# Splitting thirteen of sixteen output weight pieces in the retention and value stages of a transformer layer, with the value products grouped by high and low parts

## The chip, the cores and the metric

The kernel runs on one core of one Trainium2 chip. The metric is the device time of one execution in microseconds (us). Before the change it was measured three times: 1208.9, 1209.09 and 1209.12, median 1209.09 us.

A core has five engines with instruction streams of their own: TensorE (PE in the profile: matmuls and transposes; PEld is its loading of weights), VectorE (DVE), ScalarE (ACT), GpSimd (POOL) and SyncE (SP), which here only issues transfers. Each engine takes its instructions in the order in which they are written for it, and waits on semaphores for what the others make.

## The reference

One decoder layer over 1024 positions of width 1024, in float32. Eight heads of width 64 do causal softmax attention with a forget gate, four heads of width 128 do retention; their outputs are joined, projected by `w_out`, and a gated MLP follows.

```python
h = x * (1.0 + sc1) + sh1
proj = h @ w_in[l]
fq, fk, fv, ff, rq, rk, rv, rg = jnp.split(proj, IN_SPLITS, axis=-1)
log_f = jax.nn.log_sigmoid(ff + b_f[l])
fox = forgetting_attention(fq, fk, fv, log_f)     # softmax(q k^T * scale + cum_i - cum_j), causal
ret = retention(rq, rk, rv, rg)                   # chunks of 128, normalised, times silu(g)
mix = jnp.concatenate([fox, ret], axis=-1) @ w_out[l]
x = layer_norm(ALPHA * x + g1 * mix, ln1_g[l], ln1_b[l])
h = x * (1.0 + sc2) + sh2
u = causal_depthwise_conv(h @ w_up[l], conv_w[l], conv_b[l])
a, bv = jnp.split(u, 2, axis=-1)
y = (jax.nn.gelu(a, approximate=False) * bv) @ w_down[l]
x = layer_norm(ALPHA * x + g2 * y, ln2_g[l], ln2_b[l])
```

## The kernel before

**Split products.** A float32 product is made of several matmuls in a shorter float32 type (fp32r). An operand is split into a high part, which is the operand cast to that type, and a low part, which is the operand minus the high part; the product is high by high, high by low and low by high. The cast is usually ScalarE's and the subtraction VectorE's. So each weight that is used in this way costs one operation on each of the two engines before TensorE can have it.

**Stages.** In order of time: the first products of retention (to 49 us), the retention heads (to 222), the value projection of attention together with the forget gates (to 272), forgetting attention ("fox", eight heads, to 484), the output projection and the first normalisation (to 595), the up projection (to 989) and the down projection (to 1207).

**Retention and value stage.** A head of retention is worked through in eight chunks of 128 rows; the loop runs over `m`, the number of head and chunk together. For each chunk TensorE makes the projection (24 matmuls of 512 columns, tile rp), and between these the steps of earlier chunks are emitted: the turned queries and keys (qkT, copied by ScalarE at L434; `turned["last"]` is the last such copy), their products (pS), the decay on VectorE, the output (po), normalisation, gate, and the outputs turned back (py). They are copied by ScalarE into yt (L523) and stored to `mixR` in DRAM (L525). The value stage has sixteen quarter steps `q`, each for one block of rows and one half of the columns (tile vp); ScalarE casts the high part of the values (L698), VectorE subtracts (L699). At `q` = 8 the log of the forget gates is made on VectorE by a series (L710 to L734, result lp), at 12 it is summed by TensorE (pcum), at 13 it is turned (pcumT), split and stored to `cum_d` (L761), from where GpSimd loads it into the keys of attention (tile kc, L663).

These two stages are written inside one block that a scheduler orders by a simulated timeline; what is not fixed by data or by hand may move. `vec` and `queued` fix the order among VectorE's retention operations and some transfers; `tc.issue_after(x)` puts an instruction behind `x` on its engine. Memory comes from pools of slots: tag "S" has three slots of 4 KB per partition, of which retention uses two (trig and dec), "T" four of 2 KB.

**Forgetting attention.** A head has eight row blocks, `i`. For each one TensorE makes the scores (ps, L833 and L834), VectorE takes a running minimum (L836), ScalarE the exponentials (L843), GpSimd divides (L847), TensorE turns the result back in pieces of 128 by 128 (pt, L901), ScalarE casts the high part of the probabilities (L909) and VectorE subtracts the low part (L910). `fox_pv` multiplies these with the values in three groups of row blocks, at `i` = 2, 5 and 7 with a lag of four steps (pv, L921): a group runs over its key blocks `kb`, and for each over the parts `u`, high and low, so that the two alternate. In between, TensorE makes the projections of queries and keys for the next head (qk, L800 to L802), which ScalarE (L806, L807, L815) and VectorE (L808, L812, L816) turn into the operands qq, kk and kc, and the next weights are split (L674 and L675). The order of all this is the order in which the loop over `s_` calls the parts.

**Output weights.** `w_out` has eight row blocks of 1024 columns. It is split ahead of its use, in sixteen pieces of 128 by 512, `PIECES`: a piece is loaded (L1065), ScalarE casts the high part (L1069), VectorE subtracts in place (L1076), and two stores (L1082) put both parts into the DRAM tiles `wod`, from which `wo_load` takes them in the last head. All sixteen are done during attention. `LOWS` gives the step at which a piece's subtraction and stores come: row blocks 3 and 5 of the first seven heads, and row block 0 of heads 3 and 5 (counted from 0) as well; the load comes four steps earlier, the cast two. The cast is issued behind the last exponential, the subtraction behind the last minimum.

Of the kernel before, what the change touches and what calls it, by code (L numbers as in the profile page):

```python
# [8 lines left out]
F32 = mybir.dt.float32  # L9
# [6 lines left out]
P = 128  # L16
# [15 lines left out]
def kernel(  # L32
# [172 lines left out]
    first = [fa[0][:, :512], fa[0][:, 512:], fa[1][:, :512], fa[1][:, 512:]]  # L205
    first += [bank(f"fb{i}") for i in range(3)]
    w0 = []
    mod1 = cp.tile([P, ND, 2], F32, tag="mod1", name="mod1")

    hs = {}  # L210

    def ret_consts():
        tr = slot("S", [P, 2, NT, 64], F32, "trig")
        queued("SP", nc.sync.dma_start, tr, trig)
        rc = cp.tile([P, 3, RH], F32, tag="rc", name="rc")
        queued("SP", nc.sync.dma_start, rc, rcols)
        w1_load(2)
        dec = slot("S", [P, RH, P], F32, "dec")
        queued("SP", nc.sync.dma_start, dec, decay)
        w1_load(3)  # L220
        bfb = cp.tile([P, FH], F32, tag="bfb", name="bfb")
        queued("SP", nc.sync.dma_start, bfb, bcast_rows(b_f, FH))
        lnc = cp.tile([P, 2, ND], F32, tag="lnc", name="lnc")
        queued("SP", nc.sync.dma_start, lnc, ln1_cols)
        cw = cp.tile([P, 2 * NFF, 4], F32, tag="cw", name="cw")
        return tr, dec, rc, bfb, lnc, cw

    def h_cuts(j):
# [285 lines left out]
    def ret_out(h, half, st):  # L514
        pt = bank(f"py{h}_{half}")
        for i in range(4):
            c = half * 4 + i
            turn(
                pt[:, i * P:(i + 1) * P], st["st"][c // 2][:, c % 2, 0:P], ident
            )  # L520
        for q in range(2):
            yt = tmp([P, 256], F32, f"yt{h}_{half}_{q}")
            nc.scalar.copy(yt, pt[:, q * 256:(q + 1) * 256])  # L523
            s0 = half * 512 + q * 256
            nc.sync.dma_start(mixR[h, :, s0:s0 + 256], yt)  # L525

# [71 lines left out]
    def mod_piece():  # L598
        n = mst.get("n", 0)
        m, j = divmod(n, ND)  # L600
        if m < 4:
# [2 lines left out]
            mod_part(m, j, a)  # L604
            mst["n"] = n + 1

    ret_state(0)
    for c in range(7):
        ret_rows(0, c, first[c], sts[0])
# [6 lines left out]
    for m in range(NT - 1, RH * NT):  # L616
# [17 lines left out]
            mod_piece()  # L634
        if m > 2 * NT and c == 1:
            mod_piece()
        if m == NT + 1:
            mod_load(0)
        if 0 < h < RH - 1 and 3 <= c < 7:
# [123 lines left out]
    for q in range(2 * NT):  # L763
        n, c = 1 - q // NT, q % NT
        v_proj(c, n)
        emit(2 * RH * NT + q)
        if q < 8:
            mod_piece()
        if q in (2, 10):
            mod_rows(q // 8)  # L770
        if q == 3:
            wqk = [slot("X", [P, ND, P], F32R, f"wq{n}") for n in "hl"]
            fox_load(0)
            for half in range(2):
                fox_w(0, half)
        if q == 8:
            Lp = log_forget()
        if q == 12:
            cum = cum_forget(Lp)
        if q == 13:  # L780
            cum_store(cum)
        if q == 14:
            fox_load(1)
            fox_consts()
        if q == 15:
            T = {0: fox_alloc(0)}
# [125 lines left out]
    def fox_pv(h, g):  # L912
# [1 line left out]
        i0, i1 = SPANS[g]  # L914
        pts = PT.pop((h, g))
        pv = bank(f"pv{h}_{g}")
        for kb in range(i1 + 1):
            q0 = min(max(kb, i0), i1 - 1)
            t, at_ = where(g, kb, q0)
            for u in range(2):  # L920
                nc.tensor.matmul(  # L921
                    pv[:, (q0 - i0) * P:(i1 + 1 - i0) * P], V2[h][:, kb, :],
                    pts[t][u][:, at_:at_ + (i1 + 1 - q0) * P],
# [130 lines left out]

    wod = [dp.tile([2, P, D], F32, tag=f"wod{m}", name=f"wod{m}") for m in range(ND)]
    PIECES = [(m, slice(n, n + 512)) for m in (4, 5, 6, 7, 0, 1, 2, 3) for n in (0, 512)]
    park, wo = {}, {}

    def park_load(k):
        if k < len(PIECES):
# [129 lines left out]

    LAG = 3

    LOWS = [NT * h + i for h in range(FH - 1) for i in ((0, 3, 5) if h in (3, 5) else (3, 5))]
    LOWS = {v: k for k, v in enumerate(LOWS)}
    LOADS = {0: (4, 5), 1: (6, 7), 2: (0, 1), 3: (2, 3)}
    for part in range(4):
        fox_proj(0, T[0], 0, part)
# [697 lines left out]
```

## Time and profile before

| what | before |
|---|---|
| runs, median | 1209.09 us |
| the profiled execution | 1209.29 us |
| its span | 1207.6 us |
| TensorE busy | 1194.3 us, 99% |
| VectorE busy | 917.1 us, 76% |
| ScalarE busy | 653.2 us, 54% |
| GpSimd busy | 239.1 us, 20% |
| granted clock of TensorE | 0.998 |
| moved by DMA | 212.54 MB |

The span is the part of the execution that the profile covers; 1.69 us lie around it. "Busy" is the share of time in which an engine has an instruction at work. For TensorE this overstates the use: matmuls are pipelined and their ends are modelled, so that a stop of a few tenths of a microsecond between two matmuls can vanish under the end of the first. Such a stop is seen when starts are compared: a matmul of 512 columns is normally followed 0.23 us later. In the rows of the profile, `out<-in` are the program's tiles with their numbers left out, `x16` is a count, and in square brackets stands the idle time before an instruction and who ended it.

### The profile page before, as it was taken

The numbers are of one execution on the slowest core, as the hardware profiler recorded it, in microseconds if no ns is written. First come the engines' busy times: TensorE is split into PE (matmuls) and PEld (weight loads), VectorE is DVE, ScalarE is ACT, GpSimd is POOL, SyncE is SP. The second block draws the span as 40 slices with busy tenths as digits, with TensorE's granted clock in tenths as the row PEclk, the third lists the DMA queues.
The fourth block names the chain that finished last, engine by engine and source line by source line (L and its number), as shares of the span: only waits on it lengthen the run. The fifth ranks groups of instructions, "written<-read, shape, count | busy, mean of one in ns | idle before, by whom it ended". The sixth has DMA issues, their size and how long they took to land.

```text
span 1207.6 us, 17130 instructions
## 1 busy us (share of the span) xinstructions
PE 1194.3 (99%) x5928; PEld 1000.6 (83%) x5928; DVE 917.1 (76%) x1765; ACT 653.2 (54%) x1220; POOL 239.1 (20%) x283
## 2 busy tenths in 40 slices
PE   9999999999999999999999999999999999999997
PEld 6788888998888888888888888888888888888886
DVE  8947657767888886467998778787787876886687
ACT  6635445346777776657764545445454555543452
POOL 0015345122433343000021322211100010000021
PEclk9999999999999999999999999999999999999999
DMA  9523444613455568222278978777454489975741
GB/s 361 227 88 127 129 148 148 202 52 128 133 167 158 187 204 325 90 95 96 88 194 215 208 184 194 177 189 174 138 139 131 150 245 286 333 248 181 255 175 70
DMA packets 93511, 212.54 MB, mean 176 GB/s; under 512 B 10760, under 2 KB 17240, under 8 KB 93424
## 3 DMA queue, kind: packets, MB, share of 16 engines
q1 hardware_dynamic: 80496, 188.27, 44.8%
q0 software_dynamic: 12928, 23.17, 11.9%
q8 instruction: 47, 0.77, 0.2%
q14 instruction: 40, 0.33, 0.1%
HBM read 169.35 MB, written 76.65 MB: 204 GB/s over the span
## 4 chain that ended last, share of the span: by engine, by line
PE 92%; DVE 3%; DMA 2%; ACT 2%; issue 1%; SPq 0%; DVEq 0%; ACTq 0%
PE rp L145 11%; PE dX L1582 9%; PE dZ L1582 7%; PE uX L1358 6%; PE uX L1356 6%; PE uX L1357 6%; PE uY L1358 5%; PE uY L1357 5%; PE uY L1356 5%; PE vp L145 4%; PE pv L921 3%; PE op L184 2%; PE op L182 2%; PE op L183 2%; PE pt L901 2%; DMA ada<-in_ada_dram 2%
## 5 line engine op out<-in xcount | busy, mean ns | idle before, releaser
L145 PE MATMUL rp<-wr,hhi 128*128 128x512 f32 x400 | 127.9, 401 | 0.0
L1568 DVE TENSOR_TENSOR dl<-dr,dh 128x1024 fp32r<-128x1024 f32 x66 | 80.7, 1238 | 33.5 <-ACT dh L1556 30.9
L1185 POOL DMA_DIRECT2D sd<-gd x22 | 18.1, 821 | 396.8 <-DMA sd<-y 226.1
L847 POOL TENSOR_TENSOR S<-S,dn 128x128 f32<-128x128 f32 (+3 forms) x64 | 76.6, 1207 | 100.1 <-DVE dn L846 65.3
L1556 ACT CAST dh<-dr 128x1024 fp32r<-128x1024 f32 x58 | 59.9, 1051 | 64.0 <-DMA dr<-td 31.1
L145 PEld LDWEIGHTS rp<-wr,hhi 128*128 128x128 f32 x400 | 71.6, 189 | 12.7
L145 PE MATMUL rp<-wr,hlo 128*128 128x512 f32 x200 | 78.4, 392 | 0.0
L843 ACT ACTIVATE S<-S,mn 128x128 f32<-128x128 f32 (+3 forms) x64 | 49.9, 780 | 29.1 <-DVE mn L836 28.5
L1582 PE MATMUL dX<-dh 128*128 128x512 f32 x165 | 64.2, 389 | 0.0
L1582 PE MATMUL dX<-dl,dh 128*128 128x512 f32 x165 | 64.2, 389 | 0.0
L1582 PE MATMUL dX<-dh,dl 128*128 128x512 f32 x165 | 64.2, 389 | 0.0
L1371 ACT COPY u<-uX 128x512 f32<-128x512 f32 x44 | 25.8, 587 | 70.3 <-PE uX L1358 70.3
L145 DVE CUSTOM_DVE_ANT_0 ada<-ada,csb,cb 128x1024 f32<-128x1024 f32 x46 | 60.0, 1309 | 3.2 <-DMA ada<-in_ada_dram 2.7
L910 DVE TENSOR_TENSOR pt<-pt,pt 128x384 fp32r<-128x384 f32 (+3 forms) x104 | 50.9, 517 | 6.6 <-ACT pt L909 6.1
L800 PE MATMUL qk<-hhi,wqh 128*128 128x512 f32 x128 | 53.4, 417 | 0.0
L1582 PE MATMUL dZ<-dh 128*128 128x512 f32 x132 | 51.6, 391 | 0.0
L801 PE MATMUL qk<-hlo,wqh 128*128 128x512 f32 x128 | 51.5, 402 | 0.0
L1582 PE MATMUL dZ<-dl,dh 128*128 128x512 f32 x132 | 51.4, 389 | 0.0
L1582 PE MATMUL dZ<-dh,dl 128*128 128x512 f32 x132 | 51.4, 389 | 0.0
L802 PE MATMUL qk<-hhi,wql 128*128 128x512 f32 x128 | 51.1, 399 | 0.0
L182 PE MATMUL op<-wo,mxs 128*128 128x512 f32 x128 | 50.8, 397 | 0.0
L184 PE MATMUL op<-wo,mxs 128*128 128x512 f32 x128 | 50.1, 391 | 0.0
(1080 smaller groups left out, 3667.9 us busy)
## 6 DMA issues: line engine op xcount, KB each, us to landing
ada<-in_ada_dram SPq DMA_DIRECT2D x48, 512.0 KB, 3.8
td<-in_w_down_dram SPq DMA_DIRECT2D x44, 256.0 KB, 5.2
wa<-in_w_up_dram SPq DMA_DIRECT2D x22, 512.0 KB, 4.7
wb<-in_w_up_dram SPq DMA_DIRECT2D x22, 512.0 KB, 4.0
gd<-y SPq DMA_DIRECT2D x22, 512.0 KB, 2.7
sd<-y SPq DMA_DIRECT2D x44, 256.0 KB, 3.2
dr<-sd SPq DMA_DIRECT2D x44, 256.0 KB, 3.8
dr<-td SPq DMA_DIRECT2D x44, 256.0 KB, 4.2
```

The lines of the kernel that those rows point to most:

```text
L145: order[key] = fn(*args, **kw)
L182: mm(pt, ahi, whi, start=start, stop=False)
L184: mm(pt, alo, whi, start=False, stop=stop)
L800: nc.tensor.matmul(pt, whi[:, j, :], hhi[j][:, sl], start=(j == 0), stop=False)
L801: nc.tensor.matmul(pt, whi[:, j, :], hlo[j][:, sl], start=False, stop=False)
L847: nc.gpsimd.tensor_tensor(out=Ssb[:, :span], in0=Ssb[:, :span], in1=den.to_broadcast([P, span]), op=ALU.mult,)
L1356: nc.tensor.matmul(pt, whi, bh, start=start, stop=False, skip_group_check=True)
L1357: nc.tensor.matmul(pt, whi, bl, start=False, stop=False, skip_group_check=True)
L1358: nc.tensor.matmul(pt, wlo, bh, start=False, stop=stop, skip_group_check=True)
L1556: nc.scalar.copy(hi, raw)
L1568: nc.vector.tensor_tensor(out=lo, in0=raw, in1=f(hi), op=ALU.subtract)
L1582: nc.tensor.matmul(pt[:, to or cols], w_[:, 0, q], m_[:, 1, cols], start=start and n_ == 0, stop=stop and n_ == 2, skip_group_check=True)
```

## The change

There are three edits.

1. The splitting of pieces 0 to 12 moves from attention into the retention and value stages. `early_parks(n)` is called once per chunk from `m` = 9 on and once per quarter step `q`, so `n` runs from 0 to 38; every three calls make one piece: load, then cast and subtraction, then the two stores. They use one buffer, the third slot of tag "S", for all thirteen pieces. The cast is issued behind the last turned query, the subtraction is queued among VectorE's retention operations. `LOWS` keeps the last three pieces, at row block 5 of head 5 and row blocks 3 and 5 of head 6.
2. In `fox_pv` the loops over the part `u` and the key block `kb` are exchanged: all products of a group with high parts come first, then all with low parts.
3. In `ret_out` the copies to yt are issued behind the last turned query.

```diff
 def ret_consts():
+        park["ret"] = slot("S", [P, 2, 512], F32, "park")
 def ret_out(h, half, st):
             yt = tmp([P, 256], F32, f"yt{h}_{half}_{q}")
-            nc.scalar.copy(yt, pt[:, q * 256:(q + 1) * 256])
+            with tc.issue_after(turned["last"].ins):
+                nc.scalar.copy(yt, pt[:, q * 256:(q + 1) * 256])
...
+    def early_park(k, step):
+        m, sl = PIECES[k]
+        t = park["ret"]
+        if step == 0:
+            nc.sync.dma_start(t[:, 1, :], w_out[m * P:(m + 1) * P, sl])
+        elif step == 1:
+            with tc.issue_after(turned["last"].ins):
+                nc.scalar.copy(t[:, 0, :].bitcast(F32R), t[:, 1, :])
+            vec(nc.vector.tensor_tensor, out=t[:, 1, :].bitcast(F32R), in0=t[:, 1, :],
+                in1=t[:, 0, :], op=ALU.subtract)
+        else:
+            for u in range(2):
+                nc.sync.dma_start(wod[m][u][:, sl], t[:, u, :])
+
+    def early_parks(n):
+        k, step = divmod(n, 3)
+        if k < EARLY:
+            early_park(k, step)
+
+    EARLY = 13
...
+        if m > NT:
+            early_parks(m - NT - 1)
...
         emit(2 * RH * NT + q)
         if q < 8:
             mod_piece()
+        early_parks((RH - 1) * NT - 1 + q)
...
         pv = bank(f"pv{h}_{g}")
-        for kb in range(i1 + 1):
-            q0 = min(max(kb, i0), i1 - 1)
-            t, at_ = where(g, kb, q0)
-            for u in range(2):
+        for u in range(2):
+            for kb in range(i1 + 1):
+                q0 = min(max(kb, i0), i1 - 1)
+                t, at_ = where(g, kb, q0)
                 nc.tensor.matmul(
...
-    LOWS = [NT * h + i for h in range(FH - 1) for i in ((0, 3, 5) if h in (3, 5) else (3, 5))]
-    LOWS = {v: k for k, v in enumerate(LOWS)}
+    LOWS = {v: EARLY + n for n, v in enumerate((NT * 5 + 5, NT * 6 + 3, NT * 6 + 5))}
```

The rest of the diff only moves the definitions of `wod`, `PIECES` and `park` ahead of the block.

On VectorE the subtraction of a piece now stands among the retention and value operations, where it did not before (rst and V are retention rows and values, vp the value products, ada and gcol a row sum of the modulation). After the change, in the value stage:

```order
L728 TENSOR_TENSOR V_6_2441<-vp_1_2542,V_6_2441 128x64
L145 TENSOR_TENSOR park<-park 128x512
L145 SCALAR_TENSOR_TENSOR rst_3_1859<-rst_3_1859 128x128
L728 TENSOR_TENSOR V_4_2439<-vp_1_2597,V_4_2439 128x64
L145 ISA ada_3_3_2587,gcol<-ada_3_3_2587,csb,cb 128x1024
```

It stands between values of two quarter steps. The places in attention and on SyncE's queue are shown in the prediction.

More of the change, by code (lines that the diff above doesn't have):

```diff
@@ L207 @@
     w0 = []
+    wod = [dp.tile([2, P, D], F32, tag=f"wod{m}", name=f"wod{m}") for m in range(ND)]
+    PIECES = [(m, slice(n, n + 512)) for m in (4, 5, 6, 7, 0, 1, 2, 3) for n in (0, 512)]
+    park = {}
     mod1 = cp.tile([P, ND, 2], F32, tag="mod1", name="mod1")
@@ L1053, in h2_split @@
         return low
-    wod = [dp.tile([2, P, D], F32, tag=f"wod{m}", name=f"wod{m}") for m in range(ND)]
-    PIECES = [(m, slice(n, n + 512)) for m in (4, 5, 6, 7, 0, 1, 2, 3) for n in (0, 512)]
-    park, wo = {}, {}
+    wo = {}
     def park_load(k):
```

## Prediction

> **What bounds the kernel now.** The page of the profile comes first: its header, its table of busy time and the first line of its chain.
>
> ```profile
> span 1207.6 us, 17130 instructions
> PE 1194.3 (99%) x5928; PEld 1000.6 (83%) x5928; DVE 917.1 (76%) x1765; ACT 653.2 (54%) x1220; POOL 239.1 (20%) x283
> PE 92%; DVE 3%; DMA 2%; ACT 2%; issue 1%; SPq 0%; DVEq 0%; ACTq 0%
> ```
>
> TensorE is the bound nearly everywhere, and the change takes no matmul away. It can only win or lose at the places where TensorE stands still, and a busy share of 99% doesn't show those, because the modelled ends of matmuls cover short stops. So I read the busy time stage by stage, then the distance between starts. In the view by windows the columns after the stretch are its length and then PE, PEld, DVE, ACT and POOL busy (with counts), clock, DMA share and GB/s.
>
> ```profile
> 52.00:120.00 68.00, 68.00 (x369) 58.38 (x368) 44.57 (x149) 28.46 (x85) 23.16 (x34) 1.00 0.29 93
> 222.00:272.00 50.00, 50.00 (x420) 49.96 (x419) 35.66 (x155) 20.16 (x86) 9.55 (x15) 1.00 0.35 117
> 272.00:484.00 212.00, 210.70 (x1180) 177.89 (x1180) 174.36 (x471) 150.33 (x357) 80.43 (x71) 1.00 0.56 185
> ```
>
> The rows are a stretch of retention, the value stage and forgetting attention. VectorE is 82% busy in attention (174.36 of 212.00) and 66 and 71% in the others; ScalarE is 71% there against 42 and 40%. Attention is also the only one of these stages in which TensorE isn't covered. The granted clock is 1.00 in all rows.
>
> What TensorE waits for in attention at the value products (L921) is asked of that line; the rows give microseconds of idle time, counted on the loading of weights, and how often:
>
> ```profile
>   DVE pt L910: 3.1, 8
>   ACT pt L909: 2.3, 7
> ```
>
> These 5.4 us bound what faster probability pieces can give at L921; part of a late weight load is covered by the matmul ahead of it.
>
> **The change part by part.** *Thirteen pieces leave attention.* The work moved is that of the tile park:
>
> ```profile
> L1065 SPq DMA_DIRECT2D park<-in_w_out_dram x16: 333/482/1218, 268.6 to 419.4; - x16
> L1069 ACT CAST park<-park x16: 602/606/628, 283.0 to 438.2; 128x512 fp32r<-128x512 f32 x16
> L1076 DVE TENSOR_TENSOR park<-park,park x16: 674/778/1339, 288.9 to 442.0; 128x512 fp32r<-128x512 f32 x16
> DMA to landing us min/median/max: 2.0/3.3/6.5
> ```
>
> A piece costs VectorE 0.78 us and ScalarE 0.61 us at the median. Thirteen take 10.1 us and 7.9 us out of attention. None of that is TensorE time; it counts where a subtract stands ahead of a low half that TensorE awaits. The first order shows this on VectorE, from the low halves of the seventh row block of the second head (pt_7; park is L1076, a running minimum of the scores is an ISA row). Before:
>
> ```order
> L808 SCALAR_TENSOR_TENSOR qq_3555<-qk_1_3725,qq_3555 64x512
> L910 TENSOR_TENSOR pt_2_0_1_3804<-pt_7_0_3842,pt_2_0_0_3803 128x4x128
> L910 TENSOR_TENSOR pt_2_1_1_3806<-pt_7_1_3849,pt_2_1_0_3805 128x4x128
> L812 TENSOR_TENSOR kc_3557<-qk_1_3725,kk_3556 64x512
> L816 CAST kk_3556<-kk_3556 64x512
> L675 TENSOR_TENSOR wql<-wqkr_3625,wqh 128x512
> L836 ISA S_3_3881,mn_3_3882<-ps_3_3883,late 128x512
> L836 ISA mn_3_3882 128x1
> L1076 TENSOR_TENSOR park_1_3733<-park_1_3733,park_0_3732 128x512
> ```
>
> After the change the same place reads:
>
> ```order
> L940 TENSOR_TENSOR pt_2_0_1_3835<-pt_7_0_3873,pt_2_0_0_3834 128x4x128
> L940 TENSOR_TENSOR pt_2_1_1_3837<-pt_7_1_3880,pt_2_1_0_3836 128x4x128
> L876 RECIPROCAL dn_2_3869<-dn_2_3869 128x1
> L919 MEMSET pt_0_0_0_3940 128x128
> L919 MEMSET pt_0_0_1_3941 128x128
> L838 SCALAR_TENSOR_TENSOR qq_3600<-qk_1_3763,qq_3600 64x512
> L842 TENSOR_TENSOR kc_3602<-qk_1_3763,kk_3601 64x512
> L846 CAST kk_3601<-kk_3601 64x512
> L704 TENSOR_TENSOR wql<-wqkr_3666,wqh 128x512
> L866 ISA S_3_3912,mn_3_3913<-ps_3_3914,late 128x512
> ```
>
> The subtract is gone, and the two low halves that the third group of value products needs now stand ahead of the turned query (qq). On TensorE the same place, up to those products (pv_2), reads before:
>
> ```order
> L834 MATMUL ps_3_3883<-kc_3557,q_0_3099 128x512
> L901 MATMUL pt_7_1_3849<-ident,S_7_3713 128x128 x4
> L800 MATMUL qk_0_3874<-hhi_162,wqh 128x512
> L801 MATMUL qk_0_3874<-hlo_178,wqh 128x512
> L802 MATMUL qk_0_3874<-hhi_162,wql 128x512
> L800 MATMUL qk_0_3874<-hhi_182,wqh 128x512
> L801 MATMUL qk_0_3874<-hlo_223,wqh 128x512
> L802 MATMUL qk_0_3874<-hhi_182,wql 128x512
> L921 MATMUL pv_2_3895<-pt_2_0_0_3803,V_1_2389 128x256
> L921 MATMUL pv_2_3895<-pt_2_0_1_3804,V_1_2389 128x256
> ```
>
> and after it:
>
> ```order
> L830 MATMUL qk_0_3905<-hhi_190,wqh 128x512
> L831 MATMUL qk_0_3905<-hlo_231,wqh 128x512
> L832 MATMUL qk_0_3905<-hhi_190,wql 128x512
> L863 MATMUL ps_3_3914<-kk_3601,qq_3600 128x512
> L864 MATMUL ps_3_3914<-kc_3602,q_0_3171 128x512
> L951 MATMUL pv_2_3922<-pt_2_0_0_3834,V_1_2436 128x256 x4
> L951 MATMUL pv_2_3922<-pt_2_1_0_3836,V_1_2436 128x256 x4
> L951 MATMUL pv_2_3922<-pt_2_0_1_3835,V_1_2436 128x256 x4
> L951 MATMUL pv_2_3922<-pt_2_1_1_3837,V_1_2436 128x256 x4
> ```
>
> A pair of score products now stands between the projection and pv_2, and the low halves come after eight high products. What each place costs is read from five pieces of the chain of waits (start, length, what) in heads without and with the stop, and from the timeline of TensorE, VectorE and GpSimd (start, length).
>
> ```profile
> 309.22 2.18 PE pv L921 x16
> 318.35 0.83 PE pv L921 x6
> 343.23 1.08 PE pv L921 x6
> 359.61 1.92 PE pv L921 x16
> 434.30 2.19 PE pv L921 x16
> ```
>
> ```profile
> 393.16 0.81 PE L921 MATMUL pv<-pt,V 128*128 128x384 f32 x2
> 443.26 0.82 PE L921 MATMUL pv<-pt,V 128*128 128x384 f32 x2
> 349.22 1.68 POOL L847 TENSOR_TENSOR S<-S,dn 128x896 f32<-128x896 f32 x1 [2.87 <-DVE dn L846]
> 350.17 1.28 DVE L1076 TENSOR_TENSOR park<-park,park 128x512 fp32r<-128x512 f32 x1
> 351.44 0.40 DVE L910 TENSOR_TENSOR pt<-pt,pt 128x256 fp32r<-128x256 f32 x1
> 351.30 0.40 PE L801 MATMUL qk<-hlo,wqh 128*128 128x512 f32 x1
> 351.53 0.39 PE L802 MATMUL qk<-hhi,wql 128*128 128x512 f32 x1
> 351.99 0.41 PE L921 MATMUL pv<-pt,V 128*128 128x384 f32 x1
> 352.24 0.34 PE L833 MATMUL ps<-kk,qq 128*128 128x384 f32 x1
> 352.41 0.34 PE L834 MATMUL ps<-kc,q 67*128 67x384 f32 x1
> 401.60 0.39 PE L802 MATMUL qk<-hhi,wql 128*128 128x512 f32 x1
> 402.12 0.41 PE L921 MATMUL pv<-pt,V 128*128 128x384 f32 x1
> ```
>
> - Third group, sixteen products: 2.18 against 1.92, so 0.26 us, in four of the eight heads, the first at 309.22 and the last at 434.30: 4 × 0.26 = 1.04. The new order covers it with a pair of score products and earlier low halves; I take 0.9, from 0 (the next wait takes its place) to 1.0.
> - First group, six products, where the second is already a low one: 1.08 against 0.83, so 0.25 us. In two more heads the first two products, at 393.16 and 443.26, take 0.81 where 0.17 + 0.34 = 0.51 is due: three heads, 0.75. With high parts first the first low product is the fourth one, which covers the stop even in the seventh head, whose piece stays. I take 0.6, from 0 to 0.75.
> - Second group: a 512-column product normally starts 0.23 us after the one before (351.30 to 351.53), but the value product came 0.46 later, and it then took 0.25 (351.99 to 352.24) where 384 columns take 0.17 (352.24 to 352.41). That is 0.31 us, behind a subtract of 1.28 us, whose end released the low half at 351.44. It happens in two heads (351.53 to 351.99, and 0.52 from 401.60 to 402.12), those with three pieces: 0.6. The pieces in question are gone from both, so I take 0.6, from 0.3 to 1.1 (small stops follow it).
> - Before the score products of each next head a stop stays:
>
> ```profile
> 296.87 0.49 PE L901 MATMUL pt<-ident,S 128*128 128x128 f32 x3
> 297.42 0.36 PE L833 MATMUL ps<-kk,qq 128*128 128x256 f32 x1
> 371.68 0.49 PE L901 MATMUL pt<-ident,S 128*128 128x128 f32 x3
> 372.25 0.35 PE L833 MATMUL ps<-kk,qq 128*128 128x256 f32 x1
> 349.95 0.82 PE L901 MATMUL pt<-ident,S 128*128 128x128 f32 x6
> 350.52 0.47 PE L801 MATMUL qk<-hlo,wqh 128*128 128x512 f32 x1
> ```
>
> Three transposes take 0.55 and 0.57 us to the next matmul in the first and the fourth head, as long as six take at 349.95: about half, 0.28, is waiting. It recurs in each head, eight times 0.28 or 2.3 us as an estimate. The wait is for a minimum on VectorE that stands behind the exponentials and the turned query. Two subtracts fewer per head, 1.6 us of VectorE, stand around that loop but are not in it, so I take 0.7 of the 2.3, from −0.6 (it absorbs part of the other gains) to 2.3.
>
> Attention gives 0.9 + 0.6 + 0.6 + 0.7 = 2.8 us, from −0.3 to 5.2 by the four ends.
>
> *Thirteen pieces enter retention and value.* Eight of them lie in the retention heads before 222 us, one per three chunks of some 7 us, so 21 us for a cycle. A cycle of the one buffer is cast, subtract, store, load: 0.61 + 0.78 + 3.3 + 3.3 = 8.0 us, so no engine is kept waiting there. On SyncE's queue the first load stands ahead of a load of retention weights; that can delay those by up to one landing, 3.3 us, but I cost it at nothing, since one transfer more on 16 engines at a share of 0.29 is small; this is held by the upper end below. The one chunk-level stop of TensorE in the whole profile is this:
>
> ```profile
> PE pS L145 <- ACT qkT L434: 0.5, 1, 0.5
> ```
>
> It waits for a copy on ScalarE; a cast of 0.61 ahead of such a copy costs 0 to 0.6, once. The other five lie in the value stage, where sixteen steps take 50 us and a piece's three 9.4. There VectorE must finish the log-forget sums (lp, L734) for the product pcum:
>
> ```profile
> 260.30 0.36 DVE L734 TENSOR_TENSOR lp<-lp,L 128x8 f32<-128x8 f32 x2
> 263.18 0.39 PE L145 MATMUL pcum<-lp,ones 128*128 128x64 f32 x2
> 270.76 0.72 POOL L663 DMA_DIRECT2D kc<-cum_d  x1 [15.88 <-DMA cum_d<-cumT]
> ```
>
> ```profile
> L833 PE MATMUL ps<-kk,qq x96: 277/356/507, 281.1 to 468.1; 128*128 128x512 f32 x40, 128*128 128x256 f32 x32, 128*128 128x384 f32 x24
> ```
>
> The sums are done at 260.66, 2.5 us ahead of the product. Four subtracts of 0.78, 3.1 us, now stand ahead of it, and part of that falls into idle time (VectorE idles 14 of the stage's 50 us). So this costs between 0 and 0.6; at the longest subtract, 1.34, four are 5.4 us and the stop 2.9. The subtract above that took 1.28 us began while a GpSimd operation ran and ended 0.55 us after it; GpSimd is busy in only 9.55 of 50 us here, so I take 0.3 for both stages, from 0 to 2.9.
>
> The Trainium skill, SBUF — State Buffer, section Who interferes with whom, says that a VectorE instruction with two SBUF inputs and a GpSimd one that reads SBUF lock each other out for the whole instruction. The subtract at 350.17 agrees. By that rule alone, each subtract at its longest, the loss would be 2.9 and the net about zero.
>
> On SyncE's queue the stores and the next load stand ahead of the write of cum_d, for which GpSimd waits. Before:
>
> ```order
> L525 DMA mixR<-yt_0_1_2890 128x256
> L596 DMA gates<-grow_2932 8x128
> L525 DMA mixR<-yt_1_0_2973 128x256
> L525 DMA mixR<-yt_1_1_2976 128x256
> L761 DMA cum_d<-cumT 64x3x128
> ```
>
> and after:
>
> ```order
> L601 DMA gates<-grow_2997 8x128
> L625 DMA wod_104<-park 128x512 x2
> L530 DMA mixR<-yt_1_0_3038 128x256
> L530 DMA mixR<-yt_1_1_3041 128x256
> L617 DMA park<-in_w_out_dram 128x512
> L625 DMA wod_105<-park 128x512 x2
> L790 DMA cum_d<-cumT 64x3x128
> ```
>
> If the last subtract is late, cum_d is. GpSimd passes that wait at 270.76 and the first scores (L833) start at 281.1, 10.3 us later, so I cost it at nothing; without that cover it would be the lateness itself, 1 to 3 us. *The copies to yt* come behind a turned query that they already followed: 0. The net is 2.8 − 0.3 = 2.5 us.
>
> **The rivals.** *A, the stops only move (no change).* After each group's stop TensorE reaches the next head's scores sooner, and these wait for the loop of exponentials and turned queries. For it speaks that the 0.28 us stop is there in all eight heads, with pieces or without; against it that heads without the 0.25 us stop don't show a longer one later. If it takes back 2.0 of the 2.1 us of the groups, and the 0.7 isn't earned, the net is 0.1 − 0.3, a loss of 0.2: time 1209.3.
>
> *B, the single buffer holds up the value stage (slower).* If the copies land at their longest, 6.5 us, a cycle is 0.6 + 0.8 + 13 = 14.4 us against 9.4, and ScalarE waits 5.0 us at each of the last three casts with the copies of values queued behind it. With landings of 5 us, 11.4, it waits 2.0 each time. It decides from landings of 4 us on; the median of 3.3 and a DMA share of 0.35 against 0.56 speak against it. Three waits of 2.0 to 5.0 are 6 to 15 us on ScalarE; if the lower end passes to TensorE less 0.4 each (the stop of the retention copy is the nearest row), the loss is 4.8, and with the 2.8 gained the time 1211.1.
>
> *C, all of it goes (faster still).* If both engines are ahead everywhere in attention, the 5.4 us at L921 vanish, less 0.3: 1204.0.
>
> *D, the change doesn't do what it says:* the first product of the third group waits for VectorE in either order if its bank is freed by a low subtract; then only the fewer pieces count, about 1.3 − 0.3: 1208.1. This lies inside A's bounds.
>
> **How the numbers follow.** The profiled execution took 1209.29 us, 0.2 above the median of the runs, 1209.09; the gain of 2.5 is taken from the median: 1206.6. A measurement of this kernel tells some 0.2%, 2.4 us, from no change, so my forecast is just on the faster side of that line. Chances: forecast 0.48 (of it 0.39 beyond the line), A with D 0.28, B 0.14, C 0.10. Faster by over 0.2% is 0.39 + 0.10 = 0.49; slower is 0.14, and 0.02 of A with a larger loss, 0.16; the rest, 0.35, is within. The range goes from a little under C, 1203.8, to a little under B, 1210.6.
>
> **What would show it.** Right: sixteen-product groups of 1.92 in all heads, six-product groups of 0.83, the second group without 0.46 before it, pcum within 0.5 us of its old place, and attention shorter by 2 to 3 us. Wrong: attention as long as before with longer stops before the scores (A), ScalarE's casts in the value stage waiting for the load and value products spread (B), or retention chunks that are longer.

## The result, and the profile after the change

The changed kernel takes 1216.15 us at the median of six runs (1215.23 to 1217.61), against 1209.12 before. The ratio is 1.0059, with a 95% interval of 1.0046 to 1.0072: it is 7 us slower, outside the predicted range and on the other side. The profiled execution after took 1216.62 us, that before 1209.29.

The page after the change, the same lines as before:

```profile
span 1214.9 us, 17125 instructions
PE 1195.5 (98%) x5928; PEld 1001.6 (82%) x5928; DVE 920.0 (76%) x1765; ACT 653.4 (54%) x1220; POOL 238.4 (20%) x283
PE 80%; DVE 7%; DMA 5%; ACT 3%; issue 2%; POOL 2%; SPq 0%; DVEq 0%; ACTq 0%; POOLq 0%
```

TensorE's busy time is the same to 1.2 us, and the span is 7.3 us longer. In the chain that ended last TensorE has lost 12 points; VectorE went from 3 to 7%, DMA from 2 to 5%, and GpSimd, which was not in it, has 2%. More of the chain now runs through VectorE and through transfers.

Where the time came from is read from the first and last starts of four kinds of matmul. In the rows below, the two times behind the durations are the first and the last start.

```profile
L145 PE MATMUL rp<-wr,hhi x400: 387/389/481, 49.8 to 225.9; 128*128 128x512 f32 x134
...
L145 PE MATMUL vp<-wv,hhi x256: 278/283/368, 226.5 to 278.1; 128*128 128x264 f32 x64, 128*128 128x256 f32 x64
...
L830 PE MATMUL qk<-hhi,wqh x128: 388/397/484, 278.3 to 462.8; 128*128 128x512 f32 x128
...
L951 PE MATMUL pv<-pt,V x272: 277/283/446, 299.6 to 492.9; 128*128 128x256 f32 x96, 128*128 128x384 f32 x40
```

Retention runs from the first rp to the first vp, the value stage to the first qk, attention to the last pv, and the rest from there to the end of the span; the first 49.4 to 50.1 us are in no column. The first three of these stood at 49.7, 221.9 and 272.2 before, the last at 485.5. To two decimals, from the starts in the traces, and for all kernels of this study:

| profiled execution | time, us | retention | value | attention | rest |
|---|---|---|---|---|---|
| before | 1209.29 | 172.27 | 50.25 | 213.32 | 722.08 |
| after | 1216.62 | 176.75 | 51.80 | 214.56 | 722.03 |
| first edit alone (e1) | 1216.83 | 179.62 | 51.42 | 212.25 | 722.06 |
| second edit alone (e2) | 1211.10 | 172.23 | 50.25 | 215.09 | 722.02 |
| no early arithmetic (e3) | 1221.20 | 182.35 | 50.25 | 214.53 | 722.28 |
| transfers put behind (e4) | 1213.02 | 173.76 | 51.48 | 214.63 | 722.01 |
| no early loads (e5) | 1211.14 | 172.81 | 50.25 | 214.47 | 721.78 |
| second edit, not in the last head (e6) | 1209.88 | 172.23 | 50.25 | 213.92 | 721.99 |
| eight early, put behind (e7) | 1210.02 | 174.29 | 50.12 | 212.29 | 722.02 |
| third edit alone (e8) | 1209.68 | 172.23 | 50.25 | 213.33 | 722.17 |
| first edit, loads on GpSimd (e9) | 1210.40 | 172.90 | 51.98 | 212.15 | 721.78 |
| eight early, loads on GpSimd, stores behind (e10) | 1211.45 | 175.26 | 50.25 | 212.38 | 722.38 |
| two early (e11) | 1210.80 | 173.06 | 50.25 | 214.16 | 722.03 |
| eight early, loads on GpSimd (e12) | 1208.93 | 172.95 | 50.25 | 212.31 | 721.98 |

After the change, retention has 4.48 us more, the value stage 1.55 and attention 1.24, in sum 7.27 of the 7.33 by which the span grew. (Executions of the kernels with early pieces scatter: e1 from 1211.51 to 1216.83, the kernel before beside it from 1209.0 to 1210.15. The profile of e1 is its slowest run, so its retention is too long for the typical run; times below are medians.)

What TensorE waits for in the changed kernel (us in total, times, longest):

```profile
PE pS L145 <- ACT qkT L438: 2.6, 2, 1.6
PE fb L147 <- DVE warm L80: 1.5, 1, 1.5
PE op L182 <- DVE pt L940: 1.2, 1, 1.2
PE pv L951 <- DVE pt L940: 0.8, 1, 0.8
PE pq L145 <- ACT rst L476: 0.7, 1, 0.7
PE py L145 <- POOL rst L516: 0.7, 2, 0.4
```

Five places are new or longer than before: in retention a copy of turned queries (2.6 us where it was 0.5), a copy of outputs and the gates; in attention a low half of probabilities, once ahead of an output product and once ahead of a value product. (The value stage isn't in these rows; it follows with e5.) What holds the copies back stands in ScalarE's rows, from 100 to 222 us, and SyncE's, from 50 to 280:

```profile
ACT wv L539 <- DMA wvr<-in_w_v_dram: 7.4, 8, 1.6
ACT wr L171 <- DMA wrr<-in_w_ret_dram: 5.9, 4, 2.0
ACT yt L528 <- DMA mixR<-yt: 1.9, 1, 1.9
```

```profile
SPq L625 <- ACT rst L483: 23.8, 5, 12.5
SPq L617 <- DMA wod<-park: 21.4, 12, 3.2
```

From 100 to 222 us, ScalarE waited 0.4 us for retention weights before and waits 5.9 now. And on SyncE's queue stand waits that did not exist: twelve of the early loads (L617) wait for the stores of the piece ahead of them, 21.4 us in sum, seven of them and 14.5 us before the value stage begins. The early stores (L625) wait too, 66.6 us in all their rows; e5 shows what that costs. One such place, on SyncE's queue after the change:

```profile
144.90 4.13 SPq L625 DMA_DIRECT2D wod<-park  x2
149.09 0.42 SPq L593 DMA_DIRECT2D ada<-in_ada_dram  x1
152.79 0.33 SPq L617 DMA_DIRECT2D park<-in_w_out_dram  x1
153.23 0.37 SPq L177 DMA_DIRECT2D wrr<-in_w_ret_dram  x1
154.79 0.80 SPq L530 DMA_DIRECT2D mixR<-yt  x2
```

and before:

```profile
145.71 0.33 SPq L588 DMA_DIRECT2D ada<-in_ada_dram  x1
148.57 0.33 SPq L177 DMA_DIRECT2D wrr<-in_w_ret_dram  x1
152.66 0.80 SPq L525 DMA_DIRECT2D mixR<-yt  x2
```

Before, the retention weights (wrr) followed their modulation row (ada) by 2.9 us. Now the park load stands between them and is issued only at 152.79, and the weights follow it 4.1 us after the row. TensorE is 2.1 us later than before at this point; the weights are 4.7 us later. ScalarE shows the arrival, GpSimd the next link:

```profile
157.12 1.14 ACT L171 CAST wr<-wrr 128x512 fp32r<-128x512 f32 x2 [1.60 <-DMA wrr<-in_w_ret_dram]
158.16 0.58 ACT L405 COPY rst<-rp 128x512 f32<-128x512 f32 x1
158.64 0.37 ACT L438 COPY qkT<-pq 128x256 f32<-128x256 f32 x1
158.91 0.88 ACT L514 ACTIVATE rst<-rst,mr,gr 128x128 f32<-128x128 f32 x2
```

```profile
160.31 0.87 POOL L413 TENSOR_TENSOR rt<-rst,trig 128x128 f32<-128x128 f32 x2
161.14 1.05 POOL L516 TENSOR_TENSOR rst<-rst 128x128 f32<-128x128 f32 x2
```

The cast waits 1.60 us for the weights, and behind it on ScalarE are queued a row copy, a copy of turned queries and two gates; GpSimd's part of the gates comes at 161.14, and the turning of the outputs (py) waits for it.

### The profile page after: what moved, and what is told of

Same layout as the page of the kernel before. It is cut to its first block, busy times and chain, and to the rows that moved or that the text cites. A ratio compares the mean times of both kernels' runs of the same rounds, so it can differ in the third digit from the quotient of the medians.

```text
span 1214.9 us, 17125 instructions
## 1 busy us (share of the span) xinstructions
PE 1195.5 (98%) x5928; PEld 1001.6 (82%) x5928; DVE 920.0 (76%) x1765; ACT 653.4 (54%) x1220; POOL 238.4 (20%) x283
## 4 chain that ended last, share of the span: by engine, by line
PE 80%; DVE 7%; DMA 5%; ACT 3%; issue 2%; POOL 2%; SPq 0%; DVEq 0%; ACTq 0%; POOLq 0%
PE dX L1609 9%; PE dZ L1609 7%; PE uX L1385 6%; PE uX L1383 6%; PE uX L1384 6%; PE rp L145 6%; PE uY L1385 5%; PE uY L1384 5%; PE uY L1383 5%; PE op L182 2%; PE op L184 2%; PE op L183 2%; PE pv L951 2%; DMA ada<-in_ada_dram 2%; PE pt L931 2%
## 5 line engine op out<-in xcount | busy, mean ns | idle before, releaser
L1583 ACT CAST dh<-dr 128x1024 fp32r<-128x1024 f32 x58 | 60.1, 1052 | 62.4 <-DMA dr<-td 27.9
L939 ACT CAST pt<-pt 128x384 fp32r<-128x384 f32 (+3 forms) x104 | 44.3, 453 | 15.7 <-PE pt L931 14.7
L182 PE MATMUL op<-wo,mxs 128*128 128x512 f32 x128 | 50.9, 398 | 1.2 <-DVE pt L940 1.2
```

The source lines that it names most:

```text
L182: mm(pt, ahi, whi, start=start, stop=False)
L1583: nc.scalar.copy(hi, raw)
```

## The experiments

Theory S after the first reading: SyncE's queue stands at early loads that wait for the stores of the same buffer, and what is queued behind, weights and yt stores, comes late. Rivals: the added casts and subtractions (E), the added bytes (B), the tied yt copies (Y).

**First edit alone (e1).** Undone are the exchange of the loops in `fox_pv` and the yt copies' tie:

```diff
-            with tc.issue_after(turned["last"].ins):
-                nc.scalar.copy(yt, pt[:, q * 256:(q + 1) * 256])
+            nc.scalar.copy(yt, pt[:, q * 256:(q + 1) * 256])
```

> Only the first edit (thirteen pieces split early); the value products alternate and the yt copies are placed as before. Theory S (SyncE's queue stands at the early loads, which wait 1 to 3 us each for the stores of the piece before in the same buffer, 21.4 us in all, so that retention weights and yt stores come late): the loss of retention and value stages, 6.1 us, stays, time 1214 to 1217. Rival Y (the yt copies, now tied behind a turned query, hold ScalarE, for example the 1.88 us at 132.44): the loss goes, time 1207 to 1210.

Measured: 1212.58 us (ratio 1.0026, 1.0014 to 1.0037). It lies between the two expectations and misses both. The loss is less than with all edits, but in its profile retention and value stage lose, and attention gains 1.07 us. They lose without the tie, so it is not the cause of that loss; whether it adds to it beside early pieces is not shown. This run alone doesn't show that S is the cause.

**Second edit alone (e2).**

```diff
-        for kb in range(i1 + 1):
...
-            for u in range(2):
+        for u in range(2):
+            for kb in range(i1 + 1):
```

> Only the second edit (high parts first). If the value order is worth what was predicted of it, 0.6 to 1.5 us, time 1207.6 to 1208.5. If the stops before the next head's scores take it back (they measure 0.30 to 0.45 after the change where they were 0.21 to 0.36), time within 0.5 of before.

Measured: 1211.17 us (1.0015, 1.0006 to 1.0024), slower than before; a miss, since neither expected a loss of this size. All of it, 1.77 us, lies in attention. The waits of TensorE in this kernel name it:

```profile
PE op L182 <- DVE pt L910: 1.2, 1, 1.2
PE ps L833 <- DVE mn L836: 1.1, 3, 0.6
```

and VectorE and GpSimd at that place:

```profile
468.54 2.56 DVE L1118 TENSOR_TENSOR mxs<-mixF,mxs 128x256 fp32r<-128x256 f32 x3
471.02 0.41 DVE L910 TENSOR_TENSOR pt<-pt,pt 128x256 fp32r<-128x256 f32 x1
```

```profile
468.76 1.72 POOL L847 TENSOR_TENSOR S<-S,dn 128x896 f32<-128x896 f32 x1 [0.92 <-DVE dn L846]
```

In the new order of the last head three subtractions for the output products stand together ahead of a low half of probabilities, for which TensorE waits. Before, one of these took 0.42 us; the three take 2.56, of which GpSimd's operation covers 1.72.

**No early arithmetic (e3).** The thirteen early casts and subtractions are left out.

```diff
-            with tc.issue_after(turned["last"].ins):
-                nc.scalar.copy(t[:, 0, :].bitcast(F32R), t[:, 1, :])
-            vec(nc.vector.tensor_tensor, out=t[:, 1, :].bitcast(F32R), in0=t[:, 1, :],
-                in1=t[:, 0, :], op=ALU.subtract)
+            pass
...
-                nc.sync.dma_start(wod[m][u][:, sl], t[:, u, :])
+                nc.sync.dma_start(wod[m][u][:, sl], t[:, 1, :])
```

> All of the change, but the thirteen early casts and subtractions are left out: both stores of a piece write the loaded weights unsplit. All early transfers stay, on the same queue. Theory S: a load still waits for the stores before it, so at least 4 of the 6.1 us stay, time 1213 to 1216. Rival E (the casts and subtractions stand in the way on ScalarE and VectorE, which work in order): the loss goes, time 1208 to 1210.

Measured: 1221.35 us (1.0101, 1.0086 to 1.0116), 5 us slower than with the arithmetic. E is out as the cause in retention, and the size is beyond what S expected, so this run is a miss for both. SyncE's rows show why:

```profile
SPq L617 <- DMA wod<-park: 36.6, 14, 5.4
...
SPq L622 <- DMA park<-in_w_out_dram: 21.7, 11, 2.8
```

Now the stores also wait on the queue for the loads: 58.3 us of such waits, all of them before the value stage, where the changed kernel has 14.5, and retention loses 10.1 us against 4.5. The value stage is back at 50.25.

**Transfers put behind (e4).** The last load of weights or modulation, or yt store, is remembered as `pins_sp[0]`:

```diff
-            nc.sync.dma_start(t[:, 1, :], w_out[m * P:(m + 1) * P, sl])
...
+                with tc.issue_after(pins_sp[0].ins):
+                    nc.sync.dma_start(t[:, 1, :], w_out[m * P:(m + 1) * P, sl])
...
-                nc.sync.dma_start(wod[m][u][:, sl], t[:, u, :])
+                with tc.issue_after(pins_sp[0].ins):
+                    nc.sync.dma_start(wod[m][u][:, sl], t[:, u, :])
```

> All of the change, with the early loads and stores put behind the last load of modulation, retention or value weights, or yt store, that is written before them on SyncE's queue, so that a load no longer stands directly behind the stores it waits for. Same work, same buffer, same bytes. Theory S: SyncE's waits for stores shrink from 21.4 us to a few, and the time falls by 3 to 6 us, to 1210 to 1213. Rival B (the 10 MB of added transfers make the weights land later whatever the queue's order: ada 4.4 us against 3.8) or E: less than 1.5 us, 1215 and more.

Measured: 1213.36 us (1.0034, 1.002 to 1.0047), 2.8 below the changed kernel, a little short of what S expected. The loads' waits for stores are half:

```profile
SPq L622 <- DMA wod<-park: 10.5, 5, 3.3
```

and retention, which has one of these five waits, of 3.3 us, loses 1.5 us. So retention's loss falls with its waits on the queue in three steps: 58.3 and 10.1, 14.5 and 4.5, 3.3 and 1.5 us. The bytes are the same in all three, so B has at most the rest. The waits aren't all that counts: e7, below, has 3.2 us of them and loses 2.0, and e10 has none and loses 3.0.

**No early loads (e5).** Only the first early load is made.

```diff
         if step == 0:
-            nc.sync.dma_start(t[:, 1, :], w_out[m * P:(m + 1) * P, sl])
+            if k == 0:
+                nc.sync.dma_start(t[:, 1, :], w_out[m * P:(m + 1) * P, sl])
```

> All of the change, but only the first of the thirteen early loads is made; the later pieces cast, subtract and store what stands in the buffer, so twelve weight pieces aren't split. Casts, subtractions and stores stay. Theory S (loads waiting for stores hold SyncE's queue): the retention stage, 176.75 us after the change against 172.27 before, falls to 172.3 to 173.5. The value stage, 51.8 against 50.25, stays near 51.5, since its loss went only when the arithmetic was left out. Rival (stores waiting for the subtraction hold the queue as much as the loads do): retention stays above 175.

Measured: 1211.07 us (1.0014, 1.0004 to 1.0023). Retention is at 172.81, as S expected. The early stores still wait 60.1 us on the queue, and casts and subtractions are all there; together they cost 0.5 us, so the rival is out for retention, and E with it. The value stage was expected to stay at 51.5 and is at 50.25: a miss. Its loss is gone without the arithmetic (e3) and without the loads (e5), so it needs both, which fits a cast that waits for its load. In the changed kernel from 222 us on:

```profile
ACT park L620 <- DMA park<-in_w_out_dram: 6.6, 4, 3.7
```

Four of the casts wait 6.6 us for their loads, with casts of values and gates behind them. The longest of these waits can be followed to TensorE:

```profile
251.47 0.62 ACT L620 CAST park<-park 128x512 fp32r<-128x512 f32 x1 [3.67 <-DMA park<-in_w_out_dram]
255.47 3.20 ACT L514 ACTIVATE rst<-rst,mr,gr 128x128 f32<-128x128 f32 x8
258.01 1.54 PE L145 MATMUL py<-ident,rst 128*128 128x128 f32 x4
```

The gates of the last head (L514) come 29.0 us into the stage, where they came after 25.1 before (at 247.01). GpSimd's part of them follows, and the turned outputs (py) wait for it one by one: at these four TensorE falls 0.9 us behind the kernel before, and at the value products that follow the remaining 0.6.

**Second edit, not in the last head (e6).**

```diff
-        for kb in range(i1 + 1):
...
-            for u in range(2):
+        turns = [(kb, u) for u in range(2) for kb in kbs_] if h < FH - 1 else [
+            (kb, u) for kb in kbs_ for u in range(2)]
+        for kb, u in turns:
```

> Only the second edit, and in the first seven heads only; the last head alternates high and low parts as before. With the edit in all heads the time is 1211.2, 1.8 above before, of which 1.38 is one stop in the last head (the second half of an output product waits for a low half behind three subtractions of the output operands on VectorE). If that stop comes with the order of the last head: it goes, time 1209.6 to 1210.2, and a rest of 0.4 comes from longer stops before the scores. Rival (the stop comes from transfers of output weights that land late): time still about 1211.

Measured: 1209.97 us (1.0008, 0.9998 to 1.0017), as expected. Attention is 213.92: the stop before the output product is gone from TensorE's waits, and 0.6 us of the second edit's loss stays, with the stops before the scores that e2 has as well (1.1 us in three).

**Eight early, put behind (e7).** As e4, with the order of value products and copies of before.

```diff
-    EARLY = 13
+    EARLY = 8
-    LOWS = {v: EARLY + n for n, v in enumerate((NT * 5 + 5, NT * 6 + 3, NT * 6 + 5))}
+    LOWS = {v: EARLY + n for n, v in enumerate([NT * h + 5 for h in range(6)] + [NT * 6 + 3, NT * 6 + 5])}
```

> Eight pieces early, in the retention heads only, with their transfers put behind the others as in the run above; eight pieces stay in attention, one per head (two in the seventh); value products and yt copies as before. If the value stage's loss is its own four or five casts and subtractions, that stage is back at 50.25 us; retention loses the 1.5 us that it lost with this order; attention gains most of the 1.07 us that leaving parks gave. Time 1209 to 1210.5. If the value stage still loses over 1 us, late transfers from retention do it.

Measured: 1210.3 us (1.0007, 0.9998 to 1.0017). The value stage is at 50.12, so its loss is that of its own pieces, and attention gains 1.03 with eight pieces gone, about as much as with thirteen. Retention loses 2.0 us, 0.5 more than expected.

**Third edit alone (e8).**

```diff
-            nc.scalar.copy(yt, pt[:, q * 256:(q + 1) * 256])
+            with tc.issue_after(turned["last"].ins):
+                nc.scalar.copy(yt, pt[:, q * 256:(q + 1) * 256])
```

> Only the third edit. As predicted, nothing: within 0.5 us of before, stages unchanged. Rival Y: retention longer by 0.6 us or more, since the copies can no longer go ahead of a turned query.

Measured: 1209.34 us (0.9999, 0.9989 to 1.0008), no change. Y is out for the tie alone; beside early pieces it was not run apart.

**First edit, loads on GpSimd (e9).** `pool_[0]` is the latest turning product of GpSimd:

```diff
-            nc.sync.dma_start(t[:, 1, :], w_out[m * P:(m + 1) * P, sl])
+            if k == 0:
+                nc.sync.dma_start(t[:, 1, :], w_out[m * P:(m + 1) * P, sl])
+            else:
+                with tc.issue_after(pool_[0].ins):
+                    nc.gpsimd.dma_start(t[:, 1, :], w_out[m * P:(m + 1) * P, sl])
```

> The first edit alone, whole (thirteen pieces, one buffer, all work done), but the early loads after the first are issued on GpSimd's queue, each behind a turning product of retention, so that their waits for the stores no longer stand on SyncE's queue. Theory S: retention, 179.6 us in the profile of the first edit alone, falls to 172.5 to 174; time 1209 to 1211. If the added transfers themselves or the engines' work were the cause, it stays above 176. Where GpSimd stands at a load now, its products for the turns and gates come late; that would be seen in the value stage, where two loads stand ahead of the last head's gates (up to 3 us).

Measured: 1210.19 us (1.0007, 0.9998 to 1.0016), against 1212.58 in e1, with all the work and all the bytes; the two intervals share only 1.0014 to 1.0016. Retention is 172.90, with 0.6 us of its loss left. On SyncE's queue at the place shown above:

```profile
146.99 0.33 SPq L629 DMA_DIRECT2D wod<-park  x1
147.37 0.42 SPq L593 DMA_DIRECT2D ada<-in_ada_dram  x1
149.45 0.79 SPq L177 DMA_DIRECT2D wrr<-in_w_ret_dram  x1
```

The weights follow their row by 2.1 us, where it was 2.9 before and 4.1 after the change. The value stage keeps a loss, 1.7 us. The gates are late again, as was feared, but not because GpSimd stands at a load: ScalarE's cast waits for its load ahead of them, as in the changed kernel.

```profile
247.83 0.62 ACT L624 CAST park<-park 128x512 fp32r<-128x512 f32 x1 [3.92 <-DMA park<-in_w_out_dram]
```

ScalarE's gates start at 251.84, 29.1 us into the stage, and GpSimd's part 0.65 us behind them, 0.57 before.

**Eight early, loads on GpSimd, stores behind (e10).** The loads of e9 in e7:

```diff
-                with tc.issue_after(pins_sp[0].ins):
-                    nc.sync.dma_start(t[:, 1, :], w_out[m * P:(m + 1) * P, sl])
+                with tc.issue_after(pool_[0].ins):
+                    nc.gpsimd.dma_start(t[:, 1, :], w_out[m * P:(m + 1) * P, sl])
```

> Eight early pieces in retention only, loads on GpSimd's queue as in the run above and stores behind the other transfers; value products and yt copies as before. Theory S: retention 172.3 to 173.3 against 174.3 with the loads on SyncE's queue, value stage 50.2, attention 212.3: time 1208.3 to 1209.3, the first that could be below before. Rival: GpSimd's products come late instead and retention stays at 174.

Measured: 1211.45 us (1.0019, 1.001 to 1.0028), a miss: retention is 175.26, longer than with the loads on SyncE. ScalarE's cast of value weights shows the place:

```profile
219.03 0.62 ACT L540 CAST wv<-wvr 128x520 fp32r<-128x520 f32 x1 [2.51 <-DMA wvr<-in_w_v_dram]
```

Two stores of a piece and a yt store stand ahead of these weights on the queue. On ScalarE the copy of turned queries comes behind this cast and the next, at 220.85, and TensorE stands for 1.6 us. In e7 the stores stand at the same place and the same cast is as late, at 219.46; but there the copy goes ahead of the next cast, at 219.99, and TensorE has no such stop. So late weights alone don't make this stop; it takes the order on ScalarE as well.

**Two early (e11).** e1 with

```diff
-    EARLY = 13
+    EARLY = 2
-    LOWS = {v: EARLY + n for n, v in enumerate((NT * 5 + 5, NT * 6 + 3, NT * 6 + 5))}
+    LOWS = {v: EARLY + n for n, v in enumerate([NT * h + i for h in range(7) for i in (3, 5)])}
```

> Two pieces only are split early, in the second retention head, where the trace after the change shows no stop; the other fourteen stay in attention, two per head, so that the two heads with three pieces lose their third. Value products and yt copies as before. Retention and value within 0.2 us of before; attention shorter by what the third pieces cost, 0.6 us by the two stops of 0.31 us: time 1208.3 to 1209. If the heads with two pieces carry the cost as well, attention is unchanged: 1209.3.

Measured: 1211.25 us (1.0015, 1.0006 to 1.0023), a miss in both parts: retention loses 0.8 us (one of the two loads still waits 1.7 us for stores), and attention loses 0.84 instead of gaining. VectorE and GpSimd at the largest stop in attention:

```profile
351.59 2.36 DVE L703 TENSOR_TENSOR wql<-wqkr,wqh 128x512 fp32r<-128x512 f32 x1
```

```profile
351.51 1.89 POOL L876 TENSOR_TENSOR S<-S,dn 128x1024 f32<-128x1024 f32 x1
```

The place of the third piece is taken by the split of the query weights (wql), which runs beside the longest operation of GpSimd and takes 2.36 us where its median is 0.69; the low halves behind it start at 353.95, and TensorE stands for 1.1 us. That the third pieces cost 0.6 us is neither borne out nor ruled out by this run.

**Eight early, loads on GpSimd (e12).** e9 with `EARLY` and `LOWS` as in e7:

```diff
-    EARLY = 13
+    EARLY = 8
-    LOWS = {v: EARLY + n for n, v in enumerate((NT * 5 + 5, NT * 6 + 3, NT * 6 + 5))}
+    LOWS = {v: EARLY + n for n, v in enumerate([NT * h + 5 for h in range(6)] + [NT * 6 + 3, NT * 6 + 5])}
```

> Eight early pieces in retention, loads on GpSimd's queue, stores where the thirteen-piece run with GpSimd loads had them (not behind the other transfers); no early work in the value stage; value products and yt copies as before. From the stages of earlier runs: retention 172.9, value 50.25, attention 212.3 against 172.27, 50.25 and 213.32: 0.4 us below before, time 1208.5 to 1209.5. If the stop of 1.76 us before a product in the last retention head returns, as with the stores put behind, time 1210.5 and more.

Measured: 1208.98 us (0.9999, 0.999 to 1.0008): all three stages as expected. Retention still has 0.7 us more, which attention's 1.0 covers: in sum nothing is lost any more, and nothing is gained that this measurement can tell.

## Why the prediction was wrong, by its steps

*"So no engine is kept waiting there."* This is the step that failed. I compared the 8.0 us of a cycle with the 21 us that three chunks have, and in retention that holds for ScalarE and VectorE. But the load of the next piece stands on SyncE's queue directly behind the stores of the last, and waits there until they have landed, not until its turn comes. The queue was taken as a place with spare time; it is an engine that works in order. I looked at it at the start, where one load was costed at nothing, and at the end for cum_d, and not at the twelve places between. The rows quoted had the number, 3.3 us from issue to landing of the park transfers, and twelve waits of up to 3.2 us came, 14.5 us of them in retention. Retention has 4.48 us more and the value stage 1.55, together 6.03, where 0.3 was taken for both and 2.9 was the upper end. That the loads' waits on the queue make the larger part of retention's loss is shown by taking the loads away (e5, 0.5 us left) and by moving them to another queue (e9, 0.6 left); the three kernels with longer and shorter waits (e3, the change, e4) agree. No rival had it: B has the load late for its own cast, but not for what is queued behind it. Of the signs of being wrong, longer retention chunks came.

*The value stage, 0 to 2.9, taken 0.3.* It measures 1.55. That this lies inside the bounds is luck, since it doesn't come by the chain that I priced: pcum starts at 269.1 against 263.0, 6.1 us later, as the stage's end is, and has no stop of its own. The 1.55 are lost ahead of it, at the turned outputs and the value products behind them; the rows after e5 and the runs e3 and e5 point to casts that wait for loads. That is rival B's mechanism. B had 4.8 us and more; the four waits are 6.6 us on ScalarE, and 1.55 reach TensorE.

*Attention, +2.8.* It measures −1.24. Two of its three group terms came: the chain of waits after the change has the groups of sixteen products and of six as

```profile
299.78 0.82 PE pv L951 x6
315.45 1.92 PE pv L951 x16
324.31 0.82 PE pv L951 x6
340.19 1.92 PE pv L951 x16
359.50 1.32 PE pv L951 x6
366.07 1.92 PE pv L951 x16
```

The first two terms were nearly right: these rows have no group of sixteen at 2.18 and no first group at 1.08, and by the starts all that is left is 0.1 us in the sixth head and 0.1 in the seventh. The third was not: at 359.50 stand the last six products of the second group of the third head. From its first product to the next matmul this group takes 3.51 us, where those of the two heads ahead of it take 2.28 and 2.29: a stop of 1.2 us, as in e11 behind a subtraction of query weights:

```profile
356.55 2.36 DVE L704 TENSOR_TENSOR wql<-wqkr,wqh 128x512 fp32r<-128x512 f32 x1
```

```profile
354.83 3.54 POOL L877 TENSOR_TENSOR S<-S,dn 128x896 f32<-128x896 f32 x2 [2.95 <-DVE dn L876]
```

The subtraction ends 0.54 us after GpSimd's pair. The prediction showed this with the piece's own subtraction, and named the Trainium skill, SBUF — State Buffer, Who interferes with whom, for it; the trace agrees a second time. But I took the lock as a price of the pieces. Here it is paid by what moved up into their place.

*The stop before the next heads' scores, 0.7 of 2.3 earned.* Wrong in sign: summed over the eight heads it is 3.0 us after the change, where the same sum is 2.4 before (from the start of the last transpose to that of the scores, less the 0.03 us of such a step without a stop). By the same count e1 has 2.4 and e2 3.6, so the second edit lengthens these stops. That is rival A's mechanism; A would take back 2.0, and 0.6 came.

*Missing altogether: the last head.* The exchange of the two loops changes the order in which operations are issued there, and one output product waits 1.2 us (e2 has it, e6 does not). I looked at the order at one head and not at the last, where other work is mixed in. So the second edit alone costs 1.77 us in attention, 1.17 of them by the last head, and the first alone gains 1.07, near what rival D gave the fewer pieces (1.3); with both, attention is 1.24 longer, 0.5 more than the two apart make.

*The copies to yt: 0.* Right for this edit alone (e8).

What stays open is how the scatter of the kernels with early pieces comes about, and with it a part of the loss: against the kernel before beside them, the medians of e1, e2 and e8 are longer by 3.2, 1.8 and 0.0 us, and all three edits together by 7.0. Attention accounts for 0.5 of the difference of 2.0; for the rest, which may lie with the tie of the copies beside early pieces, no run was made.

## What to carry to other kernels

When work moves into an idle stretch, price its transfers as instructions of the queue that issues them: a load that refills a buffer from which a store has just been issued stands for the whole landing of that store (up to 3.2 us in the changed kernel), with everything queued behind it. Ask then what is queued there and how much time it has; a queue is idle in the profile and yet late. And when operations are taken out of a place, look at what moves up into it beside the other engines' long operations.

## What the runs showed of the hardware

In the kernel before, the changed kernel, e1 and e11, every 128 by 512 subtraction of weights on VectorE (park and wql) that began in attention while a GpSimd operation ran ended 0.5 to 0.6 us after that operation: the longest took 2.36 us, in the changed kernel and in e11, where the median of the same subtraction is 0.69. Two that began 0.16 us ahead of a GpSimd operation (the kernel before and e11) took 0.67 us.

Leaving thirteen casts and thirteen subtractions out made a kernel 5 us slower (e3): in its rows, stores wait 21.7 us for loads and loads 36.6 us for stores, all on one queue, where in the changed kernel the loads' 21.4 us are the only ones of this kind.
